# The second weight matrix of a 64-expert layer in 8 KB runs, and its left operand turned by VectorE

## The chip, the cores and the metric

The program runs on one core of a Trainium2 chip. A core has five engines with instruction streams of their own: TensorE (PE, with its weight loads as PEld), VectorE (DVE), ScalarE (ACT), GpSimd (POOL) and SyncE (SP), and 16 DMA engines that move data between HBM and the on-chip SBUF. SP issues nearly all DMAs here. The metric is device time of one execution, in microseconds (us); lower is better.

## The reference, cut to what matters

Two transformer blocks for 256 tokens of width 1024, in float32. The first block (attention, gated linear attention, feed-forward) and the mixer of the second (convolution, attention) are outside the change. The change is in the last part, a mixture of 64 experts of which every token uses two:

```
def expert_block(args):
    xb, e = args
    return (jax.nn.silu(xb @ w1[e]) * (xb @ w3[e])) @ w2[e]     # w1, w3: 1024x512, w2: 512x1024
ys = lax.map(expert_block, (xs, blk_expert)).reshape(P, D)
ys = ys * row_w[:, None].astype(ys.dtype)
out = jnp.zeros((T + 1, D), ys.dtype).at[row_tok].add(ys)[:T]
```

`xb` is the block of tokens routed to expert `e`. The three matrices of an expert are 2 MB each, so 64 experts read 384 MB from HBM.

## The kernel before, in words

The program first computes the dense parts (up to about 610 us), then runs the loop over the experts, `for e in range(NE)`, line 1261. Each expert has 32 token slots (if an expert had more, a second loop at the end would do all of it again; it isn't entered here).

**Loads.** Six loads of 1 MB per expert, all issued by SP at line 748 (`load_exp`), in a fixed order: w1 and w3 for the first half of the rows, w1 and w3 for the second half, then two pieces of w2. The tiles rotate through 21 slots in SBUF (`slot_order`), so a load waits for the tile that the load 21 places earlier filled to be used up. Beside that the loads take eight completion semaphores in turn, so each also waits for the load eight places earlier to have landed. For w1 and w3 partition p of the tile holds rows 8p to 8p+7 of the matrix, and a load takes four of them: one run of 8 KB per partition in HBM, 128 runs per load. For w2 (`load2`, line 756) partition p holds rows p, 128+p, 256+p, 384+p, and a load takes 512 of the 1024 columns: four runs of 2 KB per partition, 512 runs per load. The last expert's w2 comes in three column pieces (512, 256 and 256 columns).

**One expert on TensorE**, whose order is that in which the code is written (`manual_schedule`, line 1259):

1. `up_mm` (line 1212): 128 small matmuls, 32 for each of the four w1/w3 tiles, into one PSUM tile `ph`. The 512 hidden columns lie in four groups of 128: group c sits on partitions 32c to 32c+31, whose rows are the 32 token slots.
2. `combine` of the expert before, first half of the columns (line 1242).
3. `turn` (line 1222): a transpose of the gated values `a` (128x128), against the identity; DVE copies the result from PSUM to `aT` (line 1224). After it, columns 32c to 32c+31 of `aT` hold the slots of group c, and partition p the hidden value 128c+p.
4. `combine` of the expert before, second half.
5. `turn_weights` (line 1196): two transposes of the routing weights of expert e.
6. `down_mm` (line 1232), once for each half of the output columns: four matmuls of 32 slots by 512 columns; the first call needs only the first w2 tile, the second only the second.
7. After the second and third expert of each group of four, `gather` (line 1147) for the next four experts' tokens.

Between 1 and 3 ACT computes silu (line 1216) and DVE multiplies by the other half (line 1217).

Of the kernel before, what the change touches and what calls it, by code (L numbers as in the profile page):

```python
# [9 lines left out]
F32 = mybir.dt.float32  # L10
# [7 lines left out]
S, D = 256, 1024  # L18
# [78 lines left out]
def block_kernel(ctx: ExitStack, tc: tile.TileContext, A, out, dbg=None, stop=None):  # L97
    nc = tc.nc
# [59 lines left out]
    ident = consts.tile([128, 128], F32, name="ident")  # L158
# [9 lines left out]
    for h in range(2):  # L168
        c = slice(h * 512, (h + 1) * 512)
# [198 lines left out]
    pt = pt_()  # L368
# [9 lines left out]
    py = po_()  # L378
    for t in range(2):
        nc.tensor.matmul(py[:, t * 256:(t + 1) * 256], gl[:, t * 128:(t + 1) * 128], wg2, start=True, stop=True)  # L380
    e = mix.tile([128, 512], F32, name="gle", tag="eT", bufs=2)
# [6 lines left out]
    for f in range(2):  # L388
        for t in range(2):
            nc.tensor.matmul(pb_[:, f * 256 + t * 128:f * 256 + (t + 1) * 128], la[:, t, f * 128:(f + 1) * 128], cc("tri"),  # L390
                             start=True, stop=True)
# [58 lines left out]
    pt = pt_()  # L450
# [7 lines left out]
    for t in range(2):  # L458
        pt = pt_()
# [3 lines left out]
        pt = pt_()  # L463
# [27 lines left out]
    ph = po_()  # L491
    for i, w1 in enumerate((A["cmp_w1_k"], A["cmp_w1_v"])):
        for jj in range(2):
            wt = load_raw(w1, 0, 256, f"w_c1{i}", k0=8 * jj)
            for j in range(8):
                for h in range(2):
                    c = 2 * i + h
# [4 lines left out]
    pt = pt_()  # L502
# [32 lines left out]
    pt = pt_()  # L535
# [67 lines left out]
    for p in range(4):  # L603
        po = po_()
        for t in range(2):
# [13 lines left out]
            for a in range(2):  # L619
# [13 lines left out]
                pt = pt_()  # L633
# [107 lines left out]
    def load_exp(src, shape, name):  # L741

        p, tag, _ = slots[slot_order[n_exp[0] % len(slot_order)]]
        n_exp[0] += 1
        t = p.tile(shape, F32, name=name, tag=tag)
        dst = t if len(src.shape) == 3 else t.rearrange("p k n -> p (k n)")
        with tc.issue_after(last[0]) if last else nullcontext():
            d = nc.sync.dma_start(dst, src)  # L748
        last[:] = [d.ins]
        return t  # L750
# [3 lines left out]

        return load_exp(A[n][e].rearrange("(p k) n -> p (k n)", k=8)[:, k0 * 512:(k0 + 4) * 512], [128, 4, 512], n)

    def load2(e, c0, n):
        return c0, n, load_exp(A["w2_2"][e][:, c0:c0 + n].rearrange("(k p) n -> p k n", p=128), [128, 4, n], "w2")

    W13 = [(k0, n) for k0 in (0, 4) for n in ("w1_2", "w3_2")]  # L760
    early = []
# [321 lines left out]
    def ps(name="ps"):  # L1083
        return psum.tile([128, 512], F32, name=name, tag="f", bufs=4)
# [116 lines left out]
    def up_mm(e, w13):  # L1201

        i = e % 4
        xg, oh = by_group[e // 4]
        ph = ps()
        for k0 in range(2):
            if e == 0 and k0 == 1:
                gather(xg, oh, 1)
            for u in range(2):
                for k in range(4):  # L1210
                    for c in range(4):
                        nc.tensor.matmul(ph[32 * c:32 * c + 32, u * 128:(u + 1) * 128], xg[:, 4 * k0 + k, 32 * i:32 * i + 32],  # L1212
                                         w13[2 * k0 + u][:, k, c * 128:(c + 1) * 128], start=(k0 == 0 and k == 0 and u == 0),
                                         stop=(k0 == 1 and k == 3), tile_position=(0, 32 * c), skip_group_check=True)
        a = wk.tile([128, 128], F32, name="a")
        nc.scalar.activation(a, ph[:, 0:128], AF.Silu)  # L1216
        nc.vector.tensor_mul(a, ph[:, 128:256], a)  # L1217
        return a

    def turn(a):  # L1220
        pt = ps()
        nc.tensor.transpose(pt[:, :128], a, ident)  # L1222
        aT = wk.tile([128, 128], F32, name="aT")
        nc.vector.tensor_copy(aT, pt[:, :128])  # L1224
        return aT

    def down_mm(aT, w2):

        c0, n, w = w2
        py = ps()  # L1230
        for c in range(4):
            nc.tensor.matmul(py[32 * c:32 * c + 32, :n], aT[:, 32 * c:32 * c + 32], w[:, c], start=True, stop=True,  # L1232
                             tile_position=(0, 32 * c))
        y = wk.tile([128, 512], F32, name="y", bufs=YB)
        copy(c0 // 512, y[:, :n], py[:, :n])
        return c0, n, y
# [12 lines left out]
    def finish(stage, c0, n):  # L1249
        h, o = divmod(c0, 512)  # L1250
        for t in range(2):
# [2 lines left out]
            nc.vector.tensor_add(st.rearrange(v, k=8), oacc[2 * t + h][:, o:o + n].rearrange(v, k=8), natural(t, c0, n))  # L1254
            nc.sync.dma_start(out[t * 128:(t + 1) * 128, c0:c0 + n], st)

    with tc.manual_schedule(engines={mybir.EngineType.PE}):
        before = None  # L1260
        for e in range(NE):
            end = e == NE - 1
            b, i = divmod(e, 4)
            w13 = early + [load13(e, *x) for x in W13[len(early):]]
            early = []
            w2 = [load2(e, c0, n) for c0, n in (((0, 512), (512, 256), (768, 256)) if end else ((0, 512), (512, 512)))]
            a = up_mm(e, w13)
            if before:
                combine(e - 1, before[0], before[1])
            aT = turn(a)  # L1270
            if before:
                combine(e - 1, before[0], before[2])
            swT = turn_weights(weights_by_slot(e))
            if end:
                stage = [wk.tile([128, 8, 128], F32, name="stage", tag="xg").rearrange("p k s -> p (k s)") for _ in range(2)]
                p0, p1 = down_mm(aT, w2[0]), down_mm(aT, w2[1])
                combine(e, swT, p0)
                finish(stage, *p0[:2])
                p2 = down_mm(aT, w2[2])
                for p in (p1, p2):  # L1280
                    combine(e, swT, p)
                    finish(stage, *p[:2])
                break
            before = [swT] + [down_mm(aT, w) for w in w2]
            if b + 1 < NE // 4:
                if i == 1:
                    by_group[b + 1] = (wk.tile([128, 8, 128], F32, name="xg"), onehot(b + 1))
                if i in (1, 2):
                    gather(*by_group[b + 1], i - 1)
# [105 lines left out]
```

## Time and profile before

| What | Value |
|---|---|
| Median of 3 runs | 1588.86 us (1587.38 to 1591.41) |
| The profiled execution: its own time | 1589.37 us |
| The profiled execution: span from first to last instruction | 1587.4 us |
| TensorE, VectorE, ScalarE, GpSimd busy | 86%, 36%, 25%, 8% of the span |
| Data read from HBM | 499.74 MB, 315 GB/s over the span |
| Loads at line 748 | 383 of 1 MB and 2 of 0.5 MB |
| TensorE clock granted, mean | 0.94 of 2.4 GHz |

The shares are averages over two very different stages. In the first, the dense one, the DMA engines are half idle. From about 630 us on, the expert loop, they are not. Views by stretch of time therefore say more than the totals. An idle time in brackets, such as `[1.40 <-DMA w<-in_w]`, means that the engine stood still for 1.40 us just before the instruction and that a DMA into tile `w` ended the wait.

### The profile page before, as it was taken

To read this page: it belongs to the slowest core of one execution; us is meant where nothing else is said; L and a number is where in the kernel's file an instruction comes from. 1 tells how busy PE (TensorE), PEld (TensorE's weight loads), DVE (VectorE), ACT (ScalarE), POOL (GpSimd) and SP (SyncE) were. 2 spreads that over 40 slices of the span, in tenths; PEclk is the share of its full clock that TensorE was granted. 3 is DMA by queue.
4 is the path that set the end of the run, shared out by engine and by line. 5 is a ranking of instruction groups with operands and counts; after the bars stand their busy time and mean duration, and the time that the engine had idled before them with its cause. 6 is when DMAs were issued, how large, how long until landed. Compare 5 with 4: busy or idle time off the path is not lost.

```text
span 1587.4 us, 33179 instructions
## 1 busy us (share of the span) xinstructions
PE 1369.2 (86%) x14581; PEld 987.8 (62%) x14581; DVE 577.2 (36%) x1260; ACT 403.5 (25%) x731; POOL 125.2 (8%) x125
## 2 busy tenths in 40 slices
PE   8999999999999997998778687787787778878776
PEld 7866899998999996664444354454444444444443
DVE  6676777667876554221111111111111111111111
ACT  6544556555554441110000000000000000000000
POOL 2200032222112221000000000000000000000000
PEclk9999999999999998998999989899899988998988
DMA  9531565553546579999999999999999999999996
GB/s 322 187 107 54 171 224 200 201 183 105 175 160 213 186 267 348 410 405 409 406 408 409 407 404 407 402 406 408 399 409 400 407 407 401 409 400 408 400 408 245
DMA packets 186901, 502.98 MB, mean 317 GB/s; under 512 B 12529, under 2 KB 73986, under 8 KB 153986
## 3 DMA queue, kind: packets, MB, share of 16 engines
q1 hardware_dynamic: 184242, 500.19, 82.5%
q8 instruction: 116, 1.90, 0.5%
q10 hardware_dynamic: 2512, 0.63, 0.2%
q14 instruction: 31, 0.25, 0.0%
HBM read 499.74 MB, written 1.05 MB: 315 GB/s over the span
## 4 chain that ended last, share of the span: by engine, by line
PE 53%; DMA 41%; DVE 3%; SPq 2%; issue 1%; ACT 1%; POOL 0%; DVEq 0%; ACTq 0%
DMA w<-in_w 41%; PE pf L271 11%; PE pf L809 7%; PE oacc L1242 6%; PE pf L261 6%; PE ps L1212 6%; PE acc L798 4%; PE ps L1232 3%; PE ps L1147 2%; SPq L748 2%; PE acc L261 1%; PE pc L613 1%; PE po L650 1%; PE pt L637 0%; PE pc L970 0%
## 5 line engine op out<-in xcount | busy, mean ns | idle before, releaser
L1212 PE MATMUL ps<-w,xg 128*32 128x128 f32 x8192 | 305.0, 300 | 189.8 <-DMA w<-in_w 187.8
L1212 PEld LDWEIGHTS ps<-w,xg 128*32 128x32 f32 x8192 | 238.0, 119 | 265.1 <-DMA w<-in_w 246.9
L1242 PE MATMUL oacc<-y,swT 128*128 128x512 f32 (+1 forms) x516 | 277.4, 670 | 0.9 <-ACT y L210 0.5
L1217 DVE TENSOR_TENSOR a<-ps,a 128x128 f32<-128x128 f32 x64 | 18.6, 291 | 478.9 <-ACT a L1216 478.9
L1242 PEld LDWEIGHTS oacc<-y,swT 128*128 128x128 f32 x516 | 100.4, 217 | 115.0 <-issue 113.1
L1216 ACT ACTIVATE a<-ps 128x128 f32<-128x128 f32 x64 | 17.7, 277 | 518.8 <-PE ps L1212 518.8
L1232 PE MATMUL ps<-w,aT 128*32 128x512 f32 (+1 forms) x1032 | 123.5, 595 | 1.1 <-DMA w<-in_w 0.9
L1198 ACT ACTIVATE swT<-ps 128x256 f32<-128x256 f32 x64 | 24.5, 383 | 268.1 <-PE ps L1196 268.1
L1147 PEld LDWEIGHTS ps<-oh,h3m 128*128 128x128 f32 x512 | 61.5, 197 | 26.7 <-issue 26.7
L1189 DVE TENSOR_SCALAR sw<-cst,rk,Wm 128x128 f32<-128x128 f32 x128 | 38.5, 344 | 101.4 <-PE ps L1196 101.4
L1147 PE MATMUL ps<-oh,h3m 128*128 128x128 f32 x512 | 67.6, 287 | 1.0 <-DVE oh L1139 1.0
L210 ACT ACTIVATE y<-ps 128x512 f32<-128x512 f32 (+1 forms) x65 | 38.4, 590 | 95.9 <-PE ps L1232 95.9
L1224 DVE COPY aT<-ps 128x128 f32<-128x128 f32 x64 | 18.6, 291 | 120.5 <-PE ps L1222 120.5
L1232 PEld LDWEIGHTS ps<-w,aT 128*32 128x32 f32 x1032 | 27.2, 109 | 50.8 <-issue 49.3
L212 DVE COPY y<-ps 128x512 f32<-128x512 f32 x64 | 44.3, 692 | 31.6 <-PE ps L1232 31.6
L1149 DVE TENSOR_TENSOR xg<-ps,par 128x512 f32<-128x512 f32 x32 | 22.1, 691 | 72.0 <-PE ps L1147 72.0
L839 POOL TENSOR_TENSOR g<-uc,uc 128x256 f32<-128x256 f32 x22 | 31.4, 1429 | 154.5 <-ACT uc L837 140.3
L1196 PEld LDWEIGHTS ps<-ident,sw 128*128 128x128 f32 x128 | 18.0, 141 | 33.2 <-issue 33.2
L138 DVE TENSOR_TENSOR w_downl<-w_down,w_downh 128x1024 fp32r<-128x1024 f32 x22 | 27.1, 1234 | 26.5 <-ACT w_downh L137 26.5
L798 PE MATMUL acc<-w_downh,gh 128*128 128x512 f32 x88 | 34.9, 397 | 0.0
L798 PE MATMUL acc<-w_downh,gl 128*128 128x512 f32 x88 | 34.8, 396 | 0.0
L798 PE MATMUL acc<-w_downl,gh 128*128 128x512 f32 x88 | 34.8, 395 | 0.0
(522 smaller groups left out, 2229.0 us busy)
## 6 DMA issues: line engine op xcount, KB each, us to landing
w<-in_w SPq DMA_DIRECT2D x383, 1024.0 KB, 18.5
w_up<-in_w_up SPq DMA_DIRECT2D x22, 1024.0 KB, 5.2
w_down<-in_w_down SPq DMA_DIRECT2D x11, 1024.0 KB, 5.1
w_ccx<-in_w_in SPq DMA_DIRECT2D x8, 1024.0 KB, 5.0
w_g<-in_w_in SPq DMA_DIRECT2D x8, 1024.0 KB, 5.1
w_qkv<-in_w_in SPq DMA_DIRECT2D x6, 1024.0 KB, 5.0
w_out<-in_w_out SPq DMA_DIRECT2D x4, 1024.0 KB, 5.0
w_cb<-in_w_in SPq DMA_DIRECT2D x4, 1024.0 KB, 4.9
```

Of the source, the lines that this page charges most:

```text
L210: nc.scalar.activation(o, a, AF.Copy, scale=1.0 if scale is None else scale)
L212: nc.vector.tensor_copy(o, a)
L261: nc.tensor.matmul(o, xp[a][:, k0 + k, t * 128:(t + 1) * 128], wp[b][:, k], start=(first and j == 0 and n == 0), stop=(last and j == len(p ...
L271: nc.tensor.matmul(o, wp[b][:, k], xp[a][:, k], start=(n == 0), stop=(n == 23))
L748: d = nc.sync.dma_start(dst, src)
L798: nc.tensor.matmul(acc[2 * t + h], gp[a][:, t * 128:(t + 1) * 128], wd[b_][:, 0, h * 512:(h + 1) * 512], start=(ch == 0 and i == 0), stop= ...
L809: nc.tensor.matmul(pu[:, u * 256:(u + 1) * 256], cur[u][b_][:, k], hp[a][:, k], start=(kh == 0 and u == 0 and i == 0 and k == 0), stop=(i ...
L1147: nc.tensor.matmul(pg[:, k * 128:(k + 1) * 128], h3m[:, t, 4 * k4 + k], oh[:, t].rearrange("p e s -> p (e s)"), start=(t == 0), stop=(t == 1))
L1189: nc.vector.tensor_scalar(sw[:, t], io32[:, None, :].to_broadcast([128, 4, 32]), rk[:, t, e:e + 1], Wm[:, t, e:e + 1], op0=OP.is_equal, op ...
L1212: nc.tensor.matmul(ph[32 * c:32 * c + 32, u * 128:(u + 1) * 128], xg[:, 4 * k0 + k, 32 * i:32 * i + 32], w13[2 * k0 + u][:, k, c * 128:(c ...
L1232: nc.tensor.matmul(py[32 * c:32 * c + 32, :n], aT[:, 32 * c:32 * c + 32], w[:, c], start=True, stop=True, tile_position=(0, 32 * c))
L1242: nc.tensor.matmul(oacc[2 * t + h][:, o:o + n], swT[:, t], y[:, :n], start=(e == 0), stop=(e == NE - 1), skip_group_check=True)
```

## The change

w2 is loaded as w1 and w3 are: partition p holds rows 4p to 4p+3 of the matrix, and a load takes two of them in full width, so one run of 8 KB per partition. The four matmuls of `down_mm` now take the rows 4p+r for r = 0 to 3, two of them from each w2 tile; each of the two calls reads both tiles. To match, `aT` must hold hidden value 4p+r in column group r. The multiplication on DVE therefore writes its result with the columns regrouped (`ar`), and a DVE transpose turns each 32x32 block of it in place of the transpose on TensorE and the copy from PSUM. The last expert keeps column pieces, from the same new row order.

```
-    def load2(e, c0, n):
-        return c0, n, load_exp(A["w2_2"][e][:, c0:c0 + n].rearrange("(k p) n -> p k n", p=128), [128, 4, n], "w2")
+    def load2(e, j):
+        return load_exp(A["w2_2"][e].rearrange("(p k) n -> p (k n)", k=4)[:, j * 2 * D:(j + 1) * 2 * D], [128, 2, D], "w2")
+    def load2_cols(e, c0, n):
+        return load_exp(A["w2_2"][e].rearrange("(p k) n -> p k n", k=4)[:, :, c0:c0 + n], [128, 4, n], "w2")
...
         nc.scalar.activation(a, ph[:, 0:128], AF.Silu)
-        nc.vector.tensor_mul(a, ph[:, 128:256], a)
-        return a
-    def turn(a):
-        pt = ps()
-        nc.tensor.transpose(pt[:, :128], a, ident)
+        ar = wk.tile([128, 128], F32, name="ar", tag="a")
+        nc.vector.tensor_mul(ar.rearrange("p (r j) -> p j r", r=4), ph[:, 128:256].rearrange("p (j r) -> p j r", r=4),
+                             a.rearrange("p (j r) -> p j r", r=4))
         aT = wk.tile([128, 128], F32, name="aT")
-        nc.vector.tensor_copy(aT, pt[:, :128])
+        nc.vector.transpose(aT, ar)
         return aT
...
-        for c in range(4):
-            nc.tensor.matmul(py[32 * c:32 * c + 32, :n], aT[:, 32 * c:32 * c + 32], w[:, c], start=True, stop=True,
-                             tile_position=(0, 32 * c))
+        for r in range(4):
+            nc.tensor.matmul(py[32 * r:32 * r + 32, :n], aT[:, 32 * r:32 * r + 32], w(r), start=True, stop=True,
+                             tile_position=(0, 32 * r))
...
-            before = [swT] + [down_mm(aT, w) for w in w2]
+            before = [swT] + [down_mm(aT, c0, 512, lambda r: w2[r // 2][:, r % 2, c0:c0 + 512]) for c0 in (0, 512)]
```

On SP, the six loads of one expert in the middle of the loop; the last number of a row is the shape per partition (`128x2048` is one run of 2048 values, `128x4x512` four runs of 512). Before:

```order
103 L748 DMA w_2_7120<-in_w_2 128x2048
104 L748 DMA w_2_7122<-in_w_2 128x2048
105 L748 DMA w_2_7124<-in_w_2 128x2048
106 L748 DMA w_2_7126<-in_w_2 128x2048
107 L748 DMA w_7128<-in_w_2 128x4x512
108 L748 DMA w_7130<-in_w_2 128x4x512
```

And now:

```order
103 L748 DMA w_2_7116<-in_w_2 128x2048
104 L748 DMA w_2_7118<-in_w_2 128x2048
105 L748 DMA w_2_7120<-in_w_2 128x2048
106 L748 DMA w_2_7122<-in_w_2 128x2048
107 L748 DMA w_7124<-in_w_2 128x2048
108 L748 DMA w_7126<-in_w_2 128x2048
```

The places of the loads in SP's order are the same; the two w2 loads have the shape of the other four.

On TensorE, the end of one expert (`oacc` is the accumulator of the output, `sw` the routing weights, `w` the two w2 tiles). Before:

```order
1543 L1242 MATMUL oacc_6646<-y,swT 128x512
1544 L1242 MATMUL oacc_6648<-y,swT 128x512
1545 L1222 MATMUL ps<-ident,a 128x128
1546 L1242 MATMUL oacc_6647<-y,swT 128x512
1547 L1242 MATMUL oacc_6649<-y,swT 128x512
1548 L1196 MATMUL ps<-ident,sw 128x128 x2
1549 L1232 MATMUL ps<-w_7594,aT 32x512 x4
1550 L1232 MATMUL ps<-w_7596,aT 32x512 x4
```

And now:

```order
1551 L1245 MATMUL oacc_6646<-y,swT 128x512
1552 L1245 MATMUL oacc_6648<-y,swT 128x512
1553 L1245 MATMUL oacc_6647<-y,swT 128x512
1554 L1245 MATMUL oacc_6649<-y,swT 128x512
1555 L1201 MATMUL ps<-ident,sw 128x128 x2
1556 L1235 MATMUL ps<-w_7586,aT 32x512 x2
1557 L1235 MATMUL ps<-w_7588,aT 32x512 x2
1558 L1235 MATMUL ps<-w_7586,aT 32x512 x2
1559 L1235 MATMUL ps<-w_7588,aT 32x512 x2
```

The transpose of `a` is gone, and the first group of four matmuls takes two from each w2 tile.

## Rows read from the trace of the kernel before

**Rows 1.** The page: busy tenths and GB/s in 40 slices of the span

```profile
PE   8999999999999997998778687787787778878776
...
DMA  9531565553546579999999999999999999999996
GB/s 322 187 107 54 171 224 200 201 183 105 175 160 213 186 267 348 410 405 409 406 408 409 407 404 407 402 406 408 399 409 400 407 407 401 409 400 408 400 408 245
```

**Rows 2.** DMA view, 720 to 1560 us: packets, MB, share of 16 engines; issues

```profile
DMA packets 88141, 340.49 MB, mean 405 GB/s; under 512 B 5177, under 2 KB 5177, under 8 KB 60473
...
q1 hardware_dynamic: 88062, 339.28, 101.7%
...
w<-in_w SPq DMA_DIRECT2D x323, 1024.0 KB, 19.0
```

**Rows 3.** Waits, 720 to 1570 us: us in total, times, longest

```profile
PE ps L1212 <- DMA w<-in_w: 186.9, 159, 3.0
...
PE ps L1232 <- DMA w<-in_w: 0.9, 1, 0.9
```

**Rows 4.** Timeline of PE, line 1212: start us, us, instructions [idle before]

```profile
1319.27 0.97 PE L1212 MATMUL ps<-w,xg 128*32 128x128 f32 x28 [1.31 <-DMA w<-in_w]
...
1327.09 1.08 PE L1212 MATMUL ps<-w,xg 128*32 128x128 f32 x32 [0.92 <-DMA w<-in_w]
...
1329.60 1.93 PE L1212 MATMUL ps<-w,xg 128*32 128x128 f32 x32 [1.43 <-DMA w<-in_w]
...
1332.10 1.93 PE L1212 MATMUL ps<-w,xg 128*32 128x128 f32 x32 [0.57 <-DMA w<-in_w]
...
1334.59 1.86 PE L1212 MATMUL ps<-w,xg 128*32 128x128 f32 x32 [0.56 <-DMA w<-in_w]
...
1342.44 1.08 PE L1212 MATMUL ps<-w,xg 128*32 128x128 f32 x32 [0.17 <-DMA w<-in_w]
```

**Rows 5.** Windows: us, PE, PEld, DVE, ACT, POOL busy, PEclk, DMA share, GB/s

```profile
630.00:635.00 5.00, 4.11 (x88) 2.41 (x84) 1.80 (x5) 1.26 (x3) 0.00 (x0) 1.00 1.04 390
...
1300.00:1400.00 100.00, 79.30 (x1043) 47.09 (x1044) 15.09 (x42) 7.82 (x19) 0.00 (x0) 0.85 1.02 402
```

**Rows 6.** Line 748 from 500 to 640 us; then landing times, 900 to 1000 us

```profile
L748 SPq DMA_DIRECT2D w<-in_w x26: 328/378/5824, 571.6 to 637.6; - x26
...
DMA to landing us min/median/max: 13.4/19.0/22.2
```

**Rows 7.** Timeline, line 1216: silu of four experts, one per expert

```profile
637.65 0.28 ACT L1216 ACTIVATE a<-ps 128x128 f32<-128x128 f32 x1 [2.90 <-PE ps L1212]
...
712.34 0.28 ACT L1216 ACTIVATE a<-ps 128x128 f32<-128x128 f32 x1 [2.90 <-PE ps L1212]
...
743.15 0.28 ACT L1216 ACTIVATE a<-ps 128x128 f32<-128x128 f32 x1 [6.36 <-PE ps L1212]
...
1569.95 0.28 ACT L1216 ACTIVATE a<-ps 128x128 f32<-128x128 f32 x1 [9.77 <-PE ps L1212]
```

**Rows 8.** Timeline of PE, line 1212: a late arrival

```profile
1003.55 1.08 PE L1212 MATMUL ps<-w,xg 128*32 128x128 f32 x32 [1.40 <-DMA w<-in_w]
...
1007.58 1.94 PE L1212 MATMUL ps<-w,xg 128*32 128x128 f32 x32 [2.96 <-DMA w<-in_w]
```

**Rows 9.** Timeline of one expert, from the multiplication to the down matmuls

```profile
1320.73 0.29 DVE L1217 TENSOR_TENSOR a<-ps,a 128x128 f32<-128x128 f32 x1 [4.01 <-ACT a L1216]
...
1322.10 0.27 PE L1222 MATMUL ps<-ident,a 128*128 128x128 f32 x1
...
1322.41 0.29 DVE L1224 COPY aT<-ps 128x128 f32<-128x128 f32 x1 [1.39 <-PE ps L1222]
...
1324.24 1.92 PE L1232 MATMUL ps<-w,aT 128*32 128x512 f32 x16
```

**Rows 10.** The page: a wider DVE group, mean ns of one after the bar

```profile
L138 DVE TENSOR_TENSOR w_downl<-w_down,w_downh 128x1024 fp32r<-128x1024 f32 x22 | 27.1, 1234 | 26.5 <-ACT w_downh L137 26.5
```

**Rows 11.** Chain of waits in the last expert: start us, us, what

```profile
1572.75 0.11 PE ps L1222
```

More of the change, by code (lines that the diff above doesn't have):

```diff
@@ L1216, in up_mm, with down_mm @@
         nc.scalar.activation(a, ph[:, 0:128], AF.Silu)
-        nc.vector.tensor_mul(a, ph[:, 128:256], a)
-        return a
-    def turn(a):
-        pt = ps()
-        nc.tensor.transpose(pt[:, :128], a, ident)
+        ar = wk.tile([128, 128], F32, name="ar", tag="a")
+        nc.vector.tensor_mul(ar.rearrange("p (r j) -> p j r", r=4), ph[:, 128:256].rearrange("p (j r) -> p j r", r=4),
+                             a.rearrange("p (j r) -> p j r", r=4))
         aT = wk.tile([128, 128], F32, name="aT")
-        nc.vector.tensor_copy(aT, pt[:, :128])
+        nc.vector.transpose(aT, ar)
         return aT
-    def down_mm(aT, w2):
-        c0, n, w = w2
+    def down_mm(aT, c0, n, w):
         py = ps()
-        for c in range(4):
-            nc.tensor.matmul(py[32 * c:32 * c + 32, :n], aT[:, 32 * c:32 * c + 32], w[:, c], start=True, stop=True,
-                             tile_position=(0, 32 * c))
+        for r in range(4):
+            nc.tensor.matmul(py[32 * r:32 * r + 32, :n], aT[:, 32 * r:32 * r + 32], w(r), start=True, stop=True,
+                             tile_position=(0, 32 * r))
         y = wk.tile([128, 512], F32, name="y", bufs=YB)
@@ L1255, in finish @@
             nc.sync.dma_start(out[t * 128:(t + 1) * 128, c0:c0 + n], st)
+    LAST = ((0, 512), (512, 256), (768, 256))
     with tc.manual_schedule(engines={mybir.EngineType.PE}):
@@ L1265, in block_kernel @@
             early = []
-            w2 = [load2(e, c0, n) for c0, n in (((0, 512), (512, 256), (768, 256)) if end else ((0, 512), (512, 512)))]
-            a = up_mm(e, w13)
+            w2 = [load2_cols(e, *c) for c in LAST] if end else [load2(e, j) for j in range(2)]
+            aT = up_mm(e, w13)
             if before:
                 combine(e - 1, before[0], before[1])
-            aT = turn(a)
-            if before:
                 combine(e - 1, before[0], before[2])
@@ L1275, in block_kernel @@
                 stage = [wk.tile([128, 8, 128], F32, name="stage", tag="xg").rearrange("p k s -> p (k s)") for _ in range(2)]
-                p0, p1 = down_mm(aT, w2[0]), down_mm(aT, w2[1])
+                p0, p1 = [down_mm(aT, *c, lambda r: w[:, r]) for c, w in zip(LAST[:2], w2)]
                 combine(e, swT, p0)
                 finish(stage, *p0[:2])
-                p2 = down_mm(aT, w2[2])
+                p2 = down_mm(aT, *LAST[2], lambda r: w2[2][:, r])
                 for p in (p1, p2):
```

## The prediction

> **What bounds the kernel now.** I read the page's slices first, since the busy shares of the whole span mix two stages. From the sixteenth slice on (630 us) the DMA row stands at 9 to the end and the rate is flat near 405 GB/s, while PE falls to 7 or 8 [rows 1]. The DMA view of 720 to 1560 us sharpens this: the loads' queue alone takes 101.7% of the 16 engines' time at a mean of 405 GB/s [rows 2]. The waits of the same stretch say who suffers: PE's up matmuls waited 159 times, 186.9 us, for a load of w; the down matmuls waited once, 0.9 us [rows 3]. So the expert loop runs at the pace of the loads, and every load that gets shorter is worth its full difference there.
>
> How long is a load? PE starts an up matmul group when its tile lands, so the starts of groups that waited are a clock of landings. From 1327.09 to 1334.59 three w1/w3 loads land 2.51, 2.50 and 2.49 us apart; between the last of one expert and the first of the next, two w2 loads and one w1/w3 load pass in 7.82 and 7.85 us [rows 4]. These are typical: over the loop I find 100 gaps of the first kind, mean 2.507, and 15 of the second, mean 7.83. Two w2 loads thus take 7.83 - 2.507 = 5.32 us, 2.66 each: 0.155 us more than the same megabyte of w1 or w3. An undisturbed expert costs 4 x 2.507 + 5.32 = 15.35 us, and 1327.09 to 1342.44 is 15.35.
>
> Where does this pace begin? The stretch 630 to 635 us is the first in which the DMA share stays above 1.0 from there on [rows 5]; by 637.6 SP had issued 26 loads of the loop [rows 6], and two earlier ones make 28. About eight of these were still under way (a landing takes 19.0 us, over seven loads of 2.5 [rows 6]), so 20 had landed: the pace holds from load 21, the w2 of the fourth expert, on. With the last expert apart, 60 experts of 64 have both w2 loads in it.
>
> PE has room: before it had caught up with the loads, from 637.65 to 712.34 us, it did 7 experts in 74.69 us without waiting for a load worth naming, 10.67 each [rows 7]. Later, from 743.15 to 1569.95, 53 experts took 826.8 us, 15.60 each [rows 7]. That is 0.25 more than the undisturbed 15.35: about once in six experts a landing is some 1.5 us late, as at 1007.58, which comes 4.03 us after the group before it where 2.5 is normal [rows 8]. I see eight such gaps, 12 us; 53 x 0.25 gives 13.
>
> **The change part by part.** *The w2 loads.* 126 of them change from 512 runs of 2 KB to 128 runs of 8 KB, the shape and the stride (8 KB of every 16 KB) of the w1/w3 loads. SP's order, the slots and the waits are the same. So I take the w1/w3 price for them: 2.507 in place of 2.66. Per expert 2 x 0.155 = 0.31 us; over 60 experts 18.7 us, all on the path. Before that, in the first experts, landings don't set the end, and I count nothing. Faster landing cannot run the queue dry: at least 13.4 us of work lie between any issue and its landing [rows 6]. The last expert's pieces keep runs of 2 and 1 KB: nothing.
>
> Here a rule speaks against the change. The Trainium skill ("DMA: Bandwidth & Descriptors", Specifications) puts the least transfer for line rate at 512 B; by it 2 KB runs would already be at full rate and the saving would be nothing. The same page ("Why small descriptors are slow") gives a fixed cost of about 3 cycles per packet beside beats of 32 B: 67/64 for 2 KB against 259/256 for 8 KB, 3.5%, an estimate of 0.087 us per load and 10.4 us in all. The trace shows 6%, 2.66 against 2.507, in this very stream, and decides.
>
> *The turn.* 64 transposes on PE, 64 PSUM copies and 64 multiplications on DVE go; 64 multiplications with a regrouped output and 64 DVE transposes come. In a warm expert the old multiplication starts at 1320.73 and the down matmuls, the reader of `aT`, at 1324.24 [rows 9]; without the transpose PE arrives up to 0.4 us earlier, near 1323.85. That leaves 3.1 us for the two new instructions. Neither is in the trace. From below each takes no less than nothing, since PE does not wait for them. From above I take the wide DVE operation on eight times the columns, 1.23 us [rows 10]: two make 2.47, still inside 3.1. I take the like-sized 0.29 us of the old pair [rows 9], which ends them near 1321.4. Hidden at every bound; what hides them are the four `combine` matmuls that now all stand before the down matmuls. DVE's next work behind the transpose are the routing weights and the copy of y, neither due before then. The first expert has no combine in front and may wait a microsecond, but lies before the paced stretch.
>
> *Both w2 tiles for the first down matmuls.* This is the one added wait. The second tile lands 2 x 2.507 = 5.01 us after the last w1/w3 tile. In the expert at 1319.27 PE reaches the down matmuls 4.97 us after that landing [rows 4, 9], at most 0.4 less now, so it waits up to 0.45 us. Behind it on PE stand the two down calls (1.92 us [rows 9]), in half of the experts a gather, and the next expert's up matmuls, for which tiles wait then. With the wait PE needs 10.67 + 0.45 = 11.1 us of the 15.04 that the loads of an expert will take, so it has caught up before the next expert's last tile. The loads don't wait for it, with 21 slots and eight loads in flight. Cost nothing; if that cover were gone, 0.45 x 60 = 27 us.
>
> *The end.* After the last load PE sets the end, and the transpose stands in the chain there with 0.11 us [rows 11]. With its weight load I take 0.2.
>
> **Sum.** The profiled execution took 1589.37 us, 2 more than its span. 1589.37 - 18.7 - 0.2 = 1570.5. The median of the three runs is 0.5 lower, 1588.86, so I forecast 1570.0. The uncertainty of the gaps (0.03 us per expert, 2 us) and of the count (1 to 4 experts, 1 us) gives 1566.5 to 1573.5 as the forecast's own range.
>
> **The rivals.** *More: the late landings go too.* If the 12 to 13 us of late landings come from the number of packets in the queue, they shrink with it: an expert has 4 x 128 + 2 x 512 = 1536 data runs and will have 768. Half of them gone gives 1564, all of them 1557. For it: I see no PE or SP event that explains them. Against: nothing shows that they follow packets rather than time or the instruction stream.
>
> *Nothing: run length is not what makes w2 slow.* If w2 loads are slower for another reason, such as their place behind four others or SP, which is held longer by loads of 512 runs, the rate stays and the time is 1588.7. Against it: SP's holding never empties the queue, the least landing time being 13.4 us [rows 6], and the loads of both kinds have the same size, tile and queue. The Trainium skill's least size for line rate ("DMA: Bandwidth & Descriptors", Specifications) would have it come out this way.
>
> *Part of it.* If only some of the difference is run length (two thirds, say, or half), 1576 to 1579.
>
> *Slower: PE becomes the bound at its low clock.* The granted clock has two levels; in 1300 to 1400 us its mean is 0.85 [rows 5], so some 30% of the time stands at half. A group of 32 matmuls then takes 1.94 instead of 1.08 us [rows 8, 4], 1.8 times. With a share f of its work at the low level, an expert takes PE 10.67 x (1 + 0.8 f). This passes the new 15.04 at f = 0.51, and the 15.60 of before, from where it is slower, at f = 0.58. Place: the new wait before the down matmuls, where PE stands idle just when it used to run. At f = 0.65 an expert takes 16.2 and the time is 1589 + 60 x 0.6 = 1625; at 0.6, 1603. Against it: a PE that is late no longer waits for tiles, and at 630 us, while it was catching up, such a PE was granted 1.00 [rows 5]. It corrects itself.
>
> **How the numbers follow.** The forecast 0.70, more 0.13, part 0.06, nothing 0.07, slower 0.04. The range 1560 to 1579 holds the forecast, the part and half of the late landings going; outside it lie nothing, slower and most of the landings going, together under 0.2. A measurement of this kernel tells about 0.3%, 5 us, from no change. Faster by more than that: forecast, more and part, 0.89; within it 0.07; slower 0.04.
>
> **What would show it.** Right: gaps of two w2 loads and one w1/w3 load at 7.5 us instead of 7.83; the mean period of an expert at 15.3 instead of 15.60; the DMA view of the loop near 413 GB/s, still above 100% share; fewer packets under 8 KB, almost none of them data; a new PE wait at the down matmuls of under half a microsecond; no DVE transpose that PE waits for after the first expert. If gaps stay at 7.83, run length was not it. If the mean period is nearer 15.04, the late landings went with the packets. I am wrong if the DMA share falls below 1 in the loop (SP or slots then hold the loads), if the w1/w3 gaps themselves grow, or if PE's groups stop showing waits for w.

## The result and the profile after

| | before | after |
|---|---|---|
| Median of 4 runs each, beside one another | 1588.12 us (1587.05 to 1591.41) | 1566.68 us (1565.75 to 1568.09) |
| Span of the profiled execution | 1587.4 us | 1566.2 us |
| TensorE clock granted, mean | 0.94 | 0.948 |

The ratio is 0.9862 (95% interval 0.9845 to 0.9879): 1.4% faster.

The page of the kernel after, busy tenths of TensorE and of the DMA engines in 40 slices of the span, and the GB/s moved:

```profile
PE   8999999999999998998787877787787877878776
...
DMA  9531465553546569999999999999999999999994
GB/s 324 190 110 55 162 210 200 195 203 119 174 150 215 184 225 356 398 417 418 419 418 418 419 417 419 419 418 419 418 418 419 418 418 419 417 417 412 418 419 183
```

The picture of [rows 1] stays: the dense part is the same, and from the sixteenth slice on the DMA row is full. Only the level moved, from about 405 to 418 GB/s. Next, the DMA view of the loop, 720 to 1540 us:

```profile
DMA packets 47215, 341.39 MB, mean 416 GB/s; under 512 B 5198, under 2 KB 5454, under 8 KB 5710
...
q1 hardware_dynamic: 47135, 340.16, 100.3%
...
w<-in_w SPq DMA_DIRECT2D x319, 1024.0 KB, 20.1
```

Against [rows 2], the same megabytes come in 47215 packets instead of 88141. The 55,300 packets from 2 KB to under 8 KB (60473 less 5177) have shrunk to 256, and the engines are as full as before. The length of a load is read as before, from the starts of up matmuls that waited for a tile (start us, us, instructions, idle time before them and what ended it):

```profile
1312.00 1.08 PE L1217 MATMUL ps<-w,xg 128*32 128x128 f32 x32 [0.68 <-DMA w<-in_w]
...
1314.50 1.08 PE L1217 MATMUL ps<-w,xg 128*32 128x128 f32 x32 [1.42 <-DMA w<-in_w]
...
1317.00 1.08 PE L1217 MATMUL ps<-w,xg 128*32 128x128 f32 x32 [1.42 <-DMA w<-in_w]
...
1324.56 1.08 PE L1217 MATMUL ps<-w,xg 128*32 128x128 f32 x32 [0.67 <-ACT y L210]
...
1326.96 1.08 PE L1217 MATMUL ps<-w,xg 128*32 128x128 f32 x32 [1.32 <-DMA w<-in_w]
...
1331.94 1.59 PE L1217 MATMUL ps<-w,xg 128*32 128x128 f32 x32 [0.67 <-DMA w<-in_w]
...
1345.46 0.75 PE L1217 MATMUL ps<-w,xg 128*32 128x128 f32 x20 [1.40 <-DMA w<-in_w]
```

The groups at 1317.00 and 1326.96 are four loads apart, two of w2, one of w1, one of w3: 9.96 us. Sixteen such gaps have a mean of 9.965, eighteen over five loads 12.468. That is 2.493 us per load for all six, where [rows 4] gave 2.507 and 2.66. The row at 1324.56 did not wait for its tile but for a copy on ScalarE, so it is no clock of landings. And 1345.46 is a late landing, like [rows 8]: 13.52 us for five loads, 1.05 too many.

The pace of whole experts, from the silu of ScalarE, the eleventh expert and the last, as in [rows 7]:

```profile
741.21 0.28 ACT L1221 ACTIVATE a<-ps 128x128 f32<-128x128 f32 x1 [9.43 <-PE ps L1217]
...
1547.57 0.28 ACT L1221 ACTIVATE a<-ps 128x128 f32<-128x128 f32 x1 [7.90 <-PE ps L1217]
```

53 experts in 806.36 us, 15.214 each, against 15.600 before: 20.4 us. The eleventh silu comes 1.9 us earlier, and from the last one to the end of the span it takes 18.6 us instead of 17.45, 1.2 more: 20.4 + 1.9 - 1.2 = 21.1, and the spans differ by 21.2.

The waits of TensorE, and of SP's queue, 720 to 1550 us (us in total, times, longest):

```profile
PE ps L1217 <- DMA w<-in_w: 163.2, 133, 2.6
...
PE ps L1235 <- DMA w<-in_w: 0.3, 1, 0.3
```

```profile
SPq L748 <- DMA w<-in_w: 684.4, 320, 3.3
```

TensorE still waits for the loads. At the first down matmuls (L1235), which now need both w2 tiles, it waited for a load once, 0.3 us, as rarely as in [rows 3]. SP now waits at each load for an older one to land. Before, from 720 to 1570 us, it waited mostly on TensorE for a tile's slot:

```profile
SPq L748 <- PE ps L1212: 396.9, 141, 10.3
...
SPq L748 <- DMA w<-in_w: 70.5, 81, 2.4
```

### The profile page after: what moved, and what is told of

It reads as the page before. It is cut to its first block, busy times and chain, and to the rows that moved or that the text cites. A ratio compares the mean times of both kernels' runs of the same rounds, so it can differ in the third digit from the quotient of the medians.

```text
span 1566.2 us, 33002 instructions
## 1 busy us (share of the span) xinstructions
PE 1361.3 (87%) x14517; PEld 987.7 (63%) x14517; DVE 583.9 (37%) x1260; ACT 403.7 (26%) x731; POOL 125.1 (8%) x125
## 3 DMA queue, kind: packets, MB, share of 16 engines
HBM read 499.74 MB, written 1.05 MB: 320 GB/s over the span
## 4 chain that ended last, share of the span: by engine, by line
DMA 53%; PE 42%; DVE 3%; issue 1%; ACT 1%; POOL 0%; SPq 0%; DVEq 0%; ACTq 0%
DMA w<-in_w 53%; PE pf L271 11%; PE pf L814 8%; PE pf L261 6%; PE acc L803 4%; PE ps L1217 2%; PE oacc L1245 2%; PE acc L261 1%; PE ps L1235 1%; PE ps L1152 1%; PE pc L613 1%; PE po L650 1%; PE pt L637 0%; PE pc L975 0%; PE pc L952 0%
## 5 line engine op out<-in xcount | busy, mean ns | idle before, releaser
L1217 PE MATMUL ps<-w,xg 128*32 128x128 f32 x8192 | 296.2, 294 | 176.7 <-DMA w<-in_w 163.2
L1217 PEld LDWEIGHTS ps<-w,xg 128*32 128x32 f32 x8192 | 233.3, 117 | 247.0 <-DMA w<-in_w 202.5
L1245 PE MATMUL oacc<-y,swT 128*128 128x512 f32 (+1 forms) x516 | 272.9, 677 | 0.9 <-ACT y L210 0.5
L1224 DVE TENSOR_TENSOR ar<-ps,a 128x128 f32<-128x128 f32 x64 | 24.2, 378 | 454.7 <-ACT a L1221 454.7
L1245 PEld LDWEIGHTS oacc<-y,swT 128*128 128x128 f32 x516 | 107.4, 221 | 131.6 <-issue 129.7
L1235 PE MATMUL ps<-w,aT 128*32 128x512 f32 (+1 forms) x1032 | 129.6, 595 | 1.7 <-issue 1.4
L1235 PEld LDWEIGHTS ps<-w,aT 128*32 128x32 f32 x1032 | 34.2, 109 | 50.5 <-issue 45.6
L138 DVE TENSOR_TENSOR w_up1l<-w_up,w_up1h 128x1024 fp32r<-128x1024 f32 x22 | 27.4, 1247 | 16.0 <-ACT w_up1h L137 16.0
```

Source lines behind the costliest of these rows:

```text
L138: eng.tensor_sub(lo, src, hi.bitcast(F32))
L1235: nc.tensor.matmul(py[32 * r:32 * r + 32, :n], aT[:, 32 * r:32 * r + 32], w(r), start=True, stop=True, tile_position=(0, 32 * r))
L1245: nc.tensor.matmul(oacc[2 * t + h][:, o:o + n], swT[:, t], y[:, :n], start=(e == 0), stop=(e == NE - 1), skip_group_check=True)
```

## The experiments

Each ran in three rounds beside the kernel before. "Pace" is the mean period of an expert over the same 53 experts (15.600 before, 15.214 after).

**One part at a time: the loads, or the turn.** e1 takes the new loads and keeps the turn on TensorE; e2 takes the turn on VectorE and the new row order and loads w2 in 2 KB runs.

```
e1   nc.vector.tensor_mul(a, ph[:, 128:256], a)
     ...
     nc.tensor.transpose(pt[:, :128], a, ident)
     nc.vector.tensor_copy(aT, pt[:, :128])
e2 - w2 = [load2_cols(e, *c) for c in LAST] if end else [load2(e, j) for j in range(2)]
e2 + w2 = [load2_cols(e, *c) for c in (LAST if end else ((0, 512), (512, 512)))]
```

> w2 in runs of 8 KB as in the changed kernel, but the gated values turned on TensorE as before. (The rows of the turned values are then in the old order, so the product with w2 is not the reference's; sizes and waits are.) Theory 'packets': the whole gain is the loads', so about 1567 us, and two w2 loads plus one w1/w3 load pass in 7.48 us. Rival 'turn': the gain came from taking the transpose off TensorE, so about 1588 us.

> The DVE turn and the new row order alone: w2 is loaded in column halves, four runs of 2 KB per partition from four neighbouring rows. Theory 'packets': as before, about 1588 us, gaps of 7.83 us. Rival 'turn': about 1567 us. Rival 'neighbours' (that the rows of a partition lie next to each other in HBM is what helps): between 1567 and 1578 us.

e1: 1566.4 us (1562.07 to 1567.65), ratio 0.985 (0.9827 to 0.9873), pace 15.219, and ten gaps of two w2 loads and one of w1 with a mean of 7.48 us, as expected. e2: 1589.18 (1585.48 to 1590.41), ratio 0.9995 (0.9985 to 1.0006), pace 15.602. e2's landings across two w2 loads, one of w1 and one of w3:

```profile
1210.74 1.94 PE L1217 MATMUL ps<-w,xg 128*32 128x128 f32 x32 [0.57 <-DMA w<-in_w]
...
1221.10 1.08 PE L1217 MATMUL ps<-w,xg 128*32 128x128 f32 x32 [0.88 <-DMA w<-in_w]
```

10.36 us where the kernel after has 9.96. The whole gain is the loads'; the turn and the row order are worth nothing either way.

**Run lengths between and beyond.** e3 is the kernel before with 4 KB runs for w2. e5 has 2 KB runs for all six loads. e7 loads w1 and w3 in one 2 MB load each, of 16 KB runs; e9 does so for w2 too.

```
e3 + load_exp(A["w2_2"][e][j * 256:(j + 1) * 256].rearrange("(k p) n -> p k n", p=128), [128, 2, D], "w2")
e5 + load_exp(A[n][e][k0 * 128:(k0 + 4) * 128].rearrange("(k p) n -> p k n", p=128), [128, 4, 512], n)
e7 + load_exp(A[n][e].rearrange("(p k) n -> p (k n)", k=8), [128, 8, 512], n)
```

> The kernel before with w2 in runs of 4 KB (whole rows p, 128+p and so on, two per load), turned on TensorE: 256 data runs per load instead of 512 or 128. Theory 'packets' with a cost per packet: of the 0.167 us between 2.66 and 2.493 us per load two thirds go, 2.55 us per load, about 1574 us. If the cost falls in proportion to the length of the run, one third goes: about 1581 us. If it is SP, held by loads of many runs, that mattered, all of it may go: about 1567 us.

> The kernel before with w1 and w3 in runs of 2 KB too (partition p takes rows p, 128+p and so on, so the rows meet the wrong columns of the tokens and the output is not the reference's; sizes and waits are). Theory 'packets': all six loads of an expert take 2.66 us, four of them 0.155 to 0.167 more than before, 0.62 to 0.67 us per expert, 37 to 41 us over 61 experts: 1626 to 1630 us, landings 2.66 us apart throughout. If something about w2's place in the order made it slow and not its runs, about 1588 us.

> The changed kernel with w1 and w3 each in one load of 2 MB, 16 KB per partition in one run; w2 as in the changed kernel; the slots are regrouped to seven of 16 KB and seven of 8 KB, and PE takes all of w1, then all of w3. Theory 'packets' with a cost per run, if a run of 16 KB stays one packet: from 2.66 us for 512 runs and 2.493 for 128, 0.43 ns per run, 64 fewer per megabyte, 0.028 us per load, 4 x 0.028 x 60 = 7 us less, and 1 to 3 us more at the end, where the last tile is twice as large: about 1562 us. If 16 KB are split into packets of 8 KB, or 8 KB runs are already at what the engines can do, no gain in the loop and the longer end: about 1568 us.

> e7_16k with w2 in one load of 2 MB and runs of 16 KB as well: every load of an expert but the last expert's w2 is 128 runs of 16 KB. For it the slots are eight of 16 KB; four small ones of the dense stage serve the last expert alone. Theory 'packets': from 2.493 to about 2.45 us per megabyte of w2, 5 us less over the loop than e7_16k's 1557.7. Against it, five megabytes less can be loaded ahead while TensorE still works on the first experts, up to 12 us if all of that was used. So 1553 us if the slots don't matter, up to 1565 if they do; the mean expert in the loop tells the two apart (below 15.04 us, or not).

e3: 1573.97 us (1571.12 to 1574.6), ratio 0.9896 (0.9878 to 0.9914), pace 15.319. Its landings across two w2 loads and one of w1:

```profile
1521.52 1.08 PE L1215 MATMUL ps<-w,xg 128*32 128x128 f32 x32 [1.42 <-DMA w<-in_w]
...
1529.10 1.08 PE L1215 MATMUL ps<-w,xg 128*32 128x128 f32 x32 [0.58 <-DMA w<-in_w]
```

Eleven such gaps have a mean of 7.575, so a w2 load takes 2.54 us. That is the load and the time expected of a fixed cost per packet (2.55 us, about 1574 us). A cost in proportion to the length (about 1581 us) and SP's holding (about 1567 us) were both off.

e5: 1640.21 us (1638.12 to 1642.16), ratio 1.0313 (1.029 to 1.0336), pace 16.492. That is more than the 1626 to 1630 expected. Its loads land 2.702 us apart (mean of 97 gaps), slower than the 2.66 on which its expectation rested. Two of the landings, and the DMA view of 720 to 1530 us:

```profile
1205.14 1.08 PE L1212 MATMUL ps<-w,xg 128*32 128x128 f32 x32 [1.14 <-DMA w<-in_w]
...
1207.83 1.08 PE L1212 MATMUL ps<-w,xg 128*32 128x128 f32 x32 [1.61 <-DMA w<-in_w]
```

```profile
DMA packets 156172, 311.13 MB, mean 384 GB/s; under 512 B 4730, under 2 KB 4730, under 8 KB 156100
```

e7: 1557.68 us (1557.29 to 1558.36), ratio 0.98 (0.978 to 0.9819), pace 15.040. It beats both kernels, and the 1562 us expected. The same view:

```profile
DMA packets 31673, 341.21 MB, mean 421 GB/s; under 512 B 3473, under 2 KB 3729, under 8 KB 3985
```

e9 has the best pace of the kernels that load everything, 14.969, and takes 1584.34 us (1582.69 to 1585.39), ratio 0.9966 (0.9955 to 0.9978), outside the 1553 to 1565 expected. The starts of w1's groups in two experts on end, 14.71 us apart as in most, give 2.452 us per MB:

```profile
1524.69 1.95 PE L1214 MATMUL ps<-w,xg 128*32 128x128 f32 x64 [0.62 <-DMA w<-in_w]
...
1539.40 1.95 PE L1214 MATMUL ps<-w,xg 128*32 128x128 f32 x64 [0.92 <-DMA w<-in_w]
```

Its gain is lost before the loop, as the windows of 560 to 600 us show (us, busy time of PE, PEld, DVE, ACT, POOL, clock, DMA share, GB/s), first e9, then the kernel after:

```profile
560.00:600.00 40.00, 40.00 (x274) 36.64 (x273) 21.61 (x23) 17.21 (x23) 11.01 (x10) 1.00 0.24 80
```

```profile
560.00:600.00 40.00, 40.00 (x278) 36.82 (x277) 22.33 (x24) 18.05 (x24) 11.99 (x11) 1.00 0.79 295
```

With eight tiles of 16 KB per partition there is little free for the loop's first loads while the dense part still holds its own tiles: from 500 to 640 us SP issues e9's first load of the loop at 609.0, that of the kernel after at 571.4. The 215 GB/s missing for 40 us are 8.6 MB, eight loads of 2.45 us; in the next 20 us another 3 MB are missing (197 against 344 GB/s).

**Do the late landings go with TensorE's instructions?** e6 leaves out three quarters of the up matmuls and changes no load.

```
-                for k in range(4):
+                for k in range(1):
```

> The changed kernel with a quarter of the up matmuls (one of four row groups per tile; the rest of the sum is left out). Loads, order and waits stay. In the changed kernel some landings come late: 1.05, 0.25 and 0.3 us, each about every 96 us, 13 us in all. Theory 'instructions': they are caused by fetches of TensorE's instructions, which pass the same DMA engines (70 of 16 KB in 820 us); with about a third of the instructions the late landings come about a third as often, the mean expert falls from 15.21 to about 15.05 us, and the time to 1557 to 1560 us. Rival 'time': they come every 96 us whatever the program does, and the time stays at 1564 to 1567 us (PE's end may be a microsecond or two shorter).

e6: 1554.03 us (1552.81 to 1555.31), ratio 0.9777 (0.9756 to 0.9797), pace 15.075. The total lies below the 1557 to 1560 expected, but not all of that is the loads: of the 14.5 us by which its span is shorter than that of the kernel after, 7.4 are the pace, and 6.1 come before the eleventh expert. The late landings add up to 5.96 us in 859 us, against 13.6 in 809 in the kernel after: 0.41 of the rate. Each of their kinds (0.64, 0.49, 0.28 and 0.15 us in e6) comes back every 228 us instead of every 96. The queue that fetches instructions, in the DMA view of 720 to 1530 us (packets, MB, share of 16 engines), first after, then e6:

```profile
q8 instruction: 69, 1.13, 0.6%
```

```profile
q8 instruction: 29, 0.48, 0.2%
```

29/69 is 0.42. So the late landings follow the number of instructions that TensorE runs, and the fetches do too. A fetch comes every 11.7 us in the kernel after and every 27.9 in e6, so that each kind of late landing comes back after about eight fetches in both, and the lateness per fetch is about 0.2 us in both. In the kernel after, the same view of 1344 to 1348 us, around the late landing at 1345.46, has one fetch:

```profile
q8 instruction: 1, 0.02, 1.6%
```

1.6% of 16 engines for 4 us is 1.0 us of one engine, and that landing was 1.05 late. But some of the fetches (one in 12 us) have no late landing beside them. That they are the cause fits the count and this size; how a fetch would delay a load was not shown, and no run removes the fetches alone.

**Why is a 2 KB piece dear?** e4 keeps the 8 KB runs in HBM but puts each 2 KB apart in SBUF, with 8 bytes between; e11 does so with 32 bytes. e8 and e10 cut pieces of 2016 bytes, e8 four in one stretch of 8 KB, e10 four that lie 4 KB apart, as the 2 KB pieces of e2 do. e12 is e10 with 1536 bytes.

```
e4  + load_exp(A["w2_2"][e].rearrange("(p k) (h n) -> p (k h) n", k=4, h=2)[:, 4 * j:4 * j + 4], None, "w2")
e4  + PITCH = 514     # e11: 520; a tile is 4 * PITCH wide, its pieces 512
e8  + ...[:, j * 2 * D:(j + 1) * 2 * D].rearrange("p (k n) -> p k n", k=4)[:, :, :504]
e10 + w2 = [load2_cols(e, *c) for c in (LAST if end else ((0, 504), (512, 504)))]
e12 + w2 = [load2_cols(e, *c) for c in (LAST if end else ((0, 384), (512, 384)))]
```

> The changed kernel, but every w2 tile has a gap of 8 bytes behind each 2 KB in SBUF: the source is still 8 KB in one piece per partition, the transfer has to go in 512 pieces of 2 KB. Theory 'packets': as before the change, about 1588 us, gaps of 7.83 us. Rival 'HBM' (what helps is that 8 KB are read from one place): as after, about 1567 us, gaps of 7.48 us.

> A cleaner form of e4_8k_hbm_2k_sbuf, whose wider tiles also cost it the loads before 600 us. The changed kernel, but of every 512 values of w2 the last 8 are not read (8 of 512 output columns are left out of the sum, except for the last expert): the reads of a partition still lie in one stretch of 8 KB, in four pieces of 2016 bytes that cannot be joined. Sizes, slots and places of the tiles are those of the changed kernel. Theory 'packets': 512 pieces per load again, 2.62 to 2.66 us per load, 1586 to 1588 us. Rival 'HBM': as the changed kernel, about 1566 us.

> e8_gap_of_32b ran at the changed kernel's pace although its w2 loads have 512 pieces, so a price per packet is not the cause. New theory 'places': what costs is every jump to another place in HBM, 512 per load in the kernel before, 128 in the changed one and in e8. Here e2_dve_turn_2k is run with e8's pieces: 2016 bytes of w2 at a time (8 of 512 output columns left out again), 4 KB apart in HBM. Theory 'places': slow, 2.6 to 2.66 us per load, mean expert 15.5 to 15.6 us, about 1585 us. Rival 'size' (that a piece of 2016 bytes is cheaper than one of 2048, wherever it lies): as e8, mean expert 15.17 us, about 1562 us.

> e4_8k_hbm_2k_sbuf with a gap of 32 bytes instead of 8 behind each 2 KB in SBUF, so that every piece starts at a multiple of 32 bytes; one of the 21 slots is given up for the room. The loads before 600 us may be lost as in e4, some 20 us, so the verdict is on the pace of the loop. Theory 'places' (8 KB in one place of HBM, so cheap), with e4 slow only for its crooked start addresses in SBUF: mean expert 15.2 us, three loads of which two are w2's in 7.48 us. If splitting into 2 KB is what costs, or e4's addresses did not matter: mean expert 15.55 us, as in e4.

> Pieces of 1536 B in place of 2016 B, at the same places: w2's row pieces carry 384 of 512 columns, so 256 of the 1024 output columns are left out of the sum. A load of 128 x 4 such pieces has 768 KB. From the runs so far a load takes 32 times (37.6 ns per KB + a) with a about 8 ns for pieces of 2048 and 4096 B and about 3 ns for 2016 B (worked out from loads of 2.66, 2.54, 2.493, 2.45 and 2.46 us for pieces of 2, 4, 8, 16 KB and 2016 B). Theory 'multiples': only pieces whose length is a multiple of 512 B pay the 8 ns; then 1536 B pays it too, a w2 load takes 2.06 us, two w2 loads and a w1 load 6.6 us, an undisturbed expert 14.1, the whole some 1515 us. Theory 'two KB': only pieces that fill 2048 B pay; then a = 3, a w2 load takes 1.90 us, the gap is 6.3, the expert 13.8, the whole some 1496 us. If TensorE becomes the bound at its lower clock, the gaps still tell, the total does not.

e4: 1611.18 us (1609.76 to 1615.1), ratio 1.0143 (1.0122 to 1.0164). The total misleads: the pace is 15.558, that of before, and so the loop is some 2 us shorter. The 25 us above that are again early loads that didn't run. e4's window:

```profile
560.00:600.00 40.00, 40.00 (x279) 36.86 (x278) 22.42 (x24) 18.29 (x25) 12.04 (x11) 1.00 0.27 86
```

e11: 1607.58 us (1606.98 to 1609.12), ratio 1.0119 (1.0102 to 1.0136), pace 15.512, with the same loss at the start (82 GB/s in that window). Its landings four loads apart:

```profile
1215.12 1.08 PE L1223 MATMUL ps<-w,xg 128*32 128x128 f32 x32 [1.37 <-DMA w<-in_w]
...
1225.44 1.08 PE L1223 MATMUL ps<-w,xg 128*32 128x128 f32 x32 [1.33 <-DMA w<-in_w]
```

10.32 us is one of the longer gaps; twenty of them, from 10.16 to 10.48, have a mean of 10.27. Less two loads of 2.493, a w2 load is 2.64. In e4 it is 2.67 (nineteen gaps, mean 10.32), in e2 2.68 (fourteen, 10.35). So a cut into 2 KB costs nearly the same whether the pieces are neighbours in HBM or not, and whether the gap in SBUF is 8 or 32 bytes.

e8: 1562.36 us (1561.11 to 1563.66), ratio 0.9831 (0.9814 to 0.9847), pace 15.175. e10: 1561.4 us (1561.19 to 1562.94), ratio 0.9828 (0.9811 to 0.9844), pace 15.188. Both have 186900 packets over the span, one fewer than the kernel before, and the pace of the kernel after. (In all they read 2 MB less, 5 us at the loop's rate.) e10's landings four loads apart:

```profile
1238.53 1.08 PE L1217 MATMUL ps<-w,xg 128*32 128x128 f32 x32 [2.36 <-DMA w<-in_w]
...
1248.43 1.08 PE L1217 MATMUL ps<-w,xg 128*32 128x128 f32 x32 [0.63 <-DMA w<-in_w]
```

9.90 us (mean of sixteen: 9.912), a w2 load of 2.463 for 1008 KB. That is 2.50 per MB: the rate of the 8 KB runs, from a quarter of their length. With e8 the equal price per packet fell, with e10 the place in HBM. The prediction's other suspect, SP, which is held longer by loads of 512 runs, falls with e8 too. SP's issues from 900 to 1000 us, the kernel before and then e8 (ns, least, median and most):

```profile
L748 SPq DMA_DIRECT2D w<-in_w x37: 328/953/9745, 899.7 to 993.4; - x37
```

```profile
L751 SPq DMA_DIRECT2D w<-in_w x41: 328/1012/9786, 899.6 to 997.3; - x41
```

SP is held as long as before, at the pace of the kernel after. e12: 1517.63 us (1516.8 to 1518.7), ratio 0.9548 (0.9531 to 0.9565), pace 14.391. Its landings:

```profile
1222.87 1.73 PE L1217 MATMUL ps<-w,xg 128*32 128x128 f32 x32 [0.55 <-DMA w<-in_w]
...
1232.02 1.08 PE L1217 MATMUL ps<-w,xg 128*32 128x128 f32 x32 [1.32 <-DMA w<-in_w]
```

9.15 us (mean of fourteen: 9.142), a load of 2.078 for 768 KB, where "multiples" expected 2.06 and "two KB" 1.90. Shared evenly by 16 engines, the time of one piece on one engine is:

| piece, bytes | load us | pieces per engine | ns per piece | less 37.6 ns per KB |
|---|---|---|---|---|
| 1536 (e12) | 2.078 | 32 | 64.9 | 8.5 |
| 2016 (e10) | 2.463 | 32 | 77.0 | 3.0 |
| 2048 (e11) | 2.64 | 32 | 82.5 | 7.3 |
| 2048 (e5, all loads) | 2.702 | 32 | 84.4 | 9.2 |
| 4096 (e3) | 2.54 | 16 | 158.8 | 8.4 |
| 8192 (after) | 2.493 | 8 | 311.6 | 10.8 |
| 16384 (e9, 14.71 us per expert) | 2.452 per MB | 4 | 613.0 | 11.4 |

The 37.6 ns per KB are about the slope between the last two rows, (613.0 - 311.6) / 8. Five lengths, all multiples of 512 bytes, lie within some 4 ns on one line: a fixed price of 7 to 11 ns per piece. 2016 bytes, the one length that is no such multiple, pays 3. Whether it is the odd length that is cheap, or something particular to 2016, one length can't tell.

## Why the prediction was right

**The forecast.** 1570.0 us, from 1566.5 to 1573.5; measured 1566.68, at the low end. That it lies within this range is partly luck, since two misses cancel: the loads gave 3.6 us more than the 18.7 forecast, the end cost 1.4 us more than forecast.

**The bound.** As read: the loop runs at the pace of the loads. e1 and e2 show it from both sides, and removing three quarters of the up matmuls (e6) won 0.14 us of 15.21 per expert.

**The w2 loads.** The mechanism was right, the size a little low: 18.7 us predicted, 20.4 measured over 53 experts plus 1.9 before the eleventh. The term was off in two places. First, w1 and w3 fell too, by 0.014 each. A likely reading, not shown by a run of its own, is that loads in flight overlap, so that part of a slow load's time shows in its neighbours' gaps. I had split the 15.35 us of an undisturbed expert as 4 x 2.507 + 2 x 2.66; with 2.493 for the four, w2 was 2.69 each, near the 2.702 of e5, where all loads are alike. The saving per expert is then 15.35 - 14.96 = 0.39, not 0.31. Second, the count of 60 experts: the 1.9 us before the eleventh are some five experts at that price, so about 58 gained. What makes a 2 KB run dear stays open: by e8 and e10 it is neither the count of pieces alone nor their distance.

**The rules against the change.** The least size for line rate in the Trainium skill ("DMA: Bandwidth & Descriptors", Specifications) would have had 2 KB runs as fast as 8 KB. The traces differ: a load took 2.66, 2.54 and 2.493 us with runs of 2, 4 and 8 KB (before, e3, after). The fixed cost per packet of the Trainium skill ("DMA: Bandwidth & Descriptors", "Why small descriptors are slow") has the right form for the multiples of 512 bytes, but the 3.5% estimated from it is too small: 2.69 against 2.493 is 7.9%. By the beats of 32 bytes in that section of the Trainium skill, an estimate for a piece of 2016 bytes is one beat in 64 less than for one of 2048, 1.6%. The traces show 77.0 against 82.5 to 84.4 ns, 7 to 9%, so the rule doesn't cover it.

**The late landings.** They stayed, as the forecast had it: 13.6 us, against the 12 to 13 estimated before. "More" fell: they did not shrink with packets. In e6 they went down with TensorE's instructions.

**The turn.** Hidden, and e2 shows it. The two new instructions, which I took as 0.29 us each and at most 1.23, are on the page and in the lines of the kernel after (busy time, mean ns of one), and answer to [rows 9]:

```profile
L1224 DVE TENSOR_TENSOR ar<-ps,a 128x128 f32<-128x128 f32 x64 | 24.2, 378 | 454.7 <-ACT a L1221 454.7
```

```profile
L1227 DVE STREAM_TRANSPOSE aT<-ar 128x128 f32<-128x128 f32 x64 | 19.9, 311 | 2.2
```

The regrouped output made the multiplication 0.09 us longer, and the DVE transpose takes about as long, 0.31 us, as the copy it replaces, 0.29.

**The added wait.** Up to 0.45 us per expert allowed, 0.3 us measured once as TensorE's own wait. Its weight loads waited there seven times, 3.7 us in all, and once 1.2 us, longer than I had allowed. It cost nothing: e8, whose first down matmuls need both tiles, has a pace of 15.175, and e10, where they need only the first, 15.188.

**The end.** -0.2 predicted, +1.2 measured. The last expert before, and then after:

```profile
1569.81 2.94 PE L1242 MATMUL oacc<-y,swT 128*128 128x512 f32 x4
...
1574.72 1.50 PE L1232 MATMUL ps<-w,aT 128*32 128x512 f32 x16
```


```profile
1545.57 1.93 PE L1217 MATMUL ps<-w,xg 128*32 128x128 f32 x32 [1.44 <-DMA w<-in_w]
1547.43 5.70 PE L1245 MATMUL oacc<-y,swT 128*128 128x512 f32 x8
...
1548.28 0.31 DVE L1227 STREAM_TRANSPOSE aT<-ar 128x128 f32<-128x128 f32 x1
...
1553.28 1.50 PE L1235 MATMUL ps<-w,aT 128*32 128x512 f32 x16
```

From the start of `combine` to the down matmuls it takes 5.85 us; before, with the transpose in it, 4.91 (1569.81 to 1574.72). The granted clock of the six microseconds there (1548 to 1554) was 0.71; before (1570 to 1576) it was 0.85. The transpose did leave the chain, but `combine` stood at a lower clock and took longer by more. The step had left the clock out. The other kernels bear this out: from the last silu to the end, e1, with the transpose on TensorE, takes 18.7 us at a clock of 0.69 in the first six of them, and e2, with it on VectorE, 17.3 at 0.83. In e4, e10 and e11, at 1.00, it is 16.5 to 16.7.

**The clock rival** did not come (its time at a share of 0.6 should read 1600, not 1603: 10.67 x 1.48 is 15.79 us per expert): in 1300 to 1400 us the clock rose from the 0.85 of [rows 5] to 0.93 while the rate went to 417 GB/s:

```profile
1300.00:1400.00 100.00, 77.47 (x1038) 44.35 (x1029) 15.96 (x41) 8.22 (x20) 0.00 (x0) 0.93 1.01 417
```

**The issues.** I had said that SP's holding never empties the queue. True, and the queue is longer now. Landing times of the loads issued from 900 to 1000 us, after, against 13.4/19.0/22.2 in [rows 6]:

```profile
DMA to landing us min/median/max: 19.6/20.1/20.9
```

## What to carry to other kernels

Where a stage is bound by loads, read the price of one load from the gaps between the waits that its landings end, and compare loads of the same bytes and other shapes: here 2, 4, 8 and 16 KB runs differ by a few per cent each, and the loop pays all of it. Check what a larger tile does to the loads that run ahead of the stage: e9 had the best pace and lost nearly all of it there, while e7 took part of the gain and kept most of its early loads (288 GB/s in the same window). And judge such a variant by the pace in the stage beside the total, since the totals of e4, e9 and e11 say nothing of the loads' price.

## What was not expected of the hardware

- Pieces of 2016 bytes, 186900 packets in all, cost about 3 ns each beside their bytes, pieces of 1536 to 16384 bytes that are multiples of 512 cost 7 to 11 ns. The cause is open. A load of all the data in pieces that are no multiples of 512 bytes was not tried.
- SP is held by the issue of a load for longer when loads have 512 runs: median 953 ns and up to 9.7 us for the 37 loads from 900 to 1000 us before, 328 ns for each of the 39 after. While the queue was full this cost nothing.
- Late landings of 1.05, 0.23 and 0.29 us come back about every 96 us each, or every eight fetches of instructions, and go down with TensorE's instruction count.
